# A hybrid block's first feed-forward: other load order, bank sharing, copy places and block sums at its head

## The chip, the cores and the metric

The kernel runs on one core of one Trainium2 chip. The metric is the device time of one execution in microseconds (us). Before the change it was 1982.98 us, the median of three runs (1982.03 to 1984.27). All details below come from one further, profiled execution.

## The reference

One layer works on 1040 tokens of 1024 values: 16 meta tokens and 1024 frames. Everything is float32.

```python
h = concat([meta, x])
h = h + 0.5 * swiglu(rmsnorm(h, ffn1_norm), ffn1_w_gate, ffn1_w_up, ffn1_w_down)
u = rmsnorm(h, mix_norm); P = u @ w_in
ya = window_sink_attention(...)         # from parts of P
yb = gated_linear_attention(...)        # from other parts of P
h = h + (sigmoid(gate_a) * (ya @ w_branch_att) + sigmoid(gate_b) * (yb @ w_branch_gla)) @ w_out
h = h + 0.5 * swiglu(rmsnorm(h, ffn2_norm), ffn2_w_gate, ffn2_w_up, ffn2_w_down)
return rmsnorm(h, final_norm)[16:]

def swiglu(x, w_gate, w_up, w_down):
    return (silu(x @ w_gate) * (x @ w_up)) @ w_down
```

The change touches only the beginning of the first feed-forward: its norm and its products with `w_gate` and `w_up` (1024 x 2816 each, so 22 column blocks of 128, numbered 0 to 21).

## The kernel before

**Arithmetic.** Each float32 operand is split into a high half (rounded to the matmul's format, by ScalarE) and a low half (what is left, by VectorE), and each product is three matmuls: high by high, high by low, low by high. A feature dimension of 1024 is eight parts of 128, numbered m or k. Weights are cut the same way: `plain_cut` writes `whi` on ScalarE (L220) and `wlo` on VectorE or, where it is told so, on GpSimd (L221).

**Column blocks 1 to 19** are made by `gate_up` with seven products for eight (a scheme like Strassen's): 24 matmuls per product, each product on sums of blocks of weights (`s` L455, `wop` L233 and L234) and of tokens. The token side has four blocks, B11 to B22, and four sums of them, T1 to T4, which `token_sums` makes once: subtractions in place in `ub` (L251 to L253, L257) and then their halves `tt` (L233, L234). After each product `pump` takes one piece of work out of the list `pending`, and lets `spare` do a turn of work for later phases: `w_out` and the first weight sums of the second feed-forward. The product results lie in tiles `pa`, `pb`, `pd` of two PSUM banks each.

**Column blocks 20 and 21** (the head) and block 0 are made plainly. The tokens form four chunks q = 0 to 3 of 256, 264, 256 and 264. Chunk 0 needs the token tiles x0 and x1, chunk 1 needs x2, x3 and the meta tokens (x8). The head is written out in a fixed order for SyncE's queue (SP), ScalarE (ACT), VectorE (DVE) and TensorE (PE):
- SP issues the loads: token tiles, block 20's weights in four pieces (`raw`, L532), block 21's weights in two (`rawx`, L212).
- `turn_x(q, m)` turns the chunk's tiles for one feature part with TensorE into a PSUM bank (`xps`, L573 and L575). For chunk 0 the parts m and m+1 share a bank; for other chunks each part has its own.
- `first_put` (chunks 0 and 1) reads that bank three times: ACT writes the high half `tb` (L585), DVE the low half (L588), and a raw copy goes to `ub`, by ACT for odd m (L587) and by DVE for even m (L590). Behind chunk 1's part the raw copy of both chunks is written to memory.
- `head_products(q, ...)` runs 16 steps for one column block and chunk, eight parts for the gate and eight for the up weights, three matmuls each (L650 to L652), into banks `pg` and `pu`. For block 20 gate and up steps alternate, for block 21 all gate steps come first. Ahead of a step, hooks from a table run other pieces: `put` (turn and halve one part of a later chunk), `square_x` (sum of squares of one token tile), `root` (their reciprocal roots, spread by a GpSimd copy, L621 to L623), `spread` (these turned into rows by TensorE, L631), `emptied` (results out of the banks, L660), `cut` (block 21's weights).

Behind the head a scheduler orders the work by itself. `more(0, ...)` makes block 0 for the chunks 2, 3, 0, 1; its results leave the banks in four `finish` steps (`m` on DVE, L760), which `token_sums` calls at four places through `between`. Then the pool of single banks is closed and two pools of two-bank tiles are opened over the same memory; the first product of `gate_up(1)` (`pb`, L472) is the first to write there.

Of the kernel before, what the change touches and what calls it, by code (L numbers as in the profile page):

```python
# [15 lines left out]
PSUM = bass.MemoryType.PSUM  # L16

P = 128
# [17 lines left out]
def hybrid_kernel(  # L36
# [136 lines left out]
    class Seven:  # L173
# [72 lines left out]

        def token_sums(self, ub, between=None):

            b11, b21, b12, b22 = ub[0][0:4], ub[0][4:8], ub[1][0:4], ub[1][4:8]
            for k in range(4):  # L250
                nc.vector.tensor_sub(b11[k], b12[k], b11[k])  # L251
                nc.vector.tensor_sub(b12[k], b22[k], b12[k])
                nc.vector.tensor_sub(b22[k], b22[k], b11[k])  # L253
            for n, bs in (("T2", b22), ("T1", b11), ("T3", b12), ("T4", b21)):
                for k in range(4):
                    if n == "T4":
                        nc.vector.tensor_sub(b21[k], b21[k], b22[k])  # L257
                    self.tops[n][k] = self.halves(self.operand(False, "tt"), bs[k])
                    if between is not None:
                        between(n, k)  # L260

# [32 lines left out]
        def pump(self):  # L294
            free = not self.pending
            if self.pending:
                self.pending.pop(0)()
            if self.spare:
                self.spare.turn(free and self.at > 1)
            self.at = (self.at + 1) % 7  # L300
# [233 lines left out]

    head_raw(0, 0)
    load_x(1, nc.sync)
    for i, k in ((1, 0), (0, 4), (1, 4)):
        head_raw(i, k)
    load_x(2, nc.sync)
    load_x(3, nc.sync)  # L540
    nc.sync.dma_start(out=xt[8][0:NM, :], in_=meta_tokens)
    head_raws += [ffn1.plain_raw(cols_view(w, HEADS[1] * P), r) for w, r in zip((ffn1_w_gate, ffn1_w_up), extra)]
    for t in range(4, 8):
# [17 lines left out]
    def turn_x(q, m):  # L561

        c, c0, n = CH[q]
        sl = slice(m * P, (m + 1) * P)
        if q == 0:
            if m % 2 == 0:
                pairs[m // 2] = bank("xps")
            ps = pairs[m // 2][:, (m % 2) * 256:(m % 2) * 256 + 256]
        else:
            ps = bank("xps")  # L570
        if n > 256:
            at = 256 - 8 * c
            nc.tensor.transpose(ps[:, at:at + NM], xt[8][0:NM, sl], ident[0:NM, 0:NM])  # L573
        for i in range(2):
            nc.tensor.transpose(ps[:, i * P:(i + 1) * P], xt[4 * c + c0 // P + i][:, sl], ident)  # L575
        return ps[:, 0:n]

    def first_put(q, m, ps):

        c, c0, n = CH[q]  # L580
        if c0 == 0:
            ub[0][m], B[0][m] = ffn1.block("ub"), ffn1.operand(True, "tb")
        g, cols = vec[:, G1 + m:G1 + m + 1], slice(c0, c0 + n)
        hi, lo = B[0][m][:, cols], B[0][m][:, N1 + c0:N1 + c0 + n]
        nc.scalar.activation(hi, ps, AF.Copy, scale=g)  # L585
        if m % 2:
            nc.scalar.copy(ub[0][m][:, cols], ps)  # L587
        nc.vector.scalar_tensor_tensor(lo, ps, g, hi.bitcast(F32), op0=ALU.mult, op1=ALU.subtract)  # L588
        if m % 2 == 0:
            nc.vector.tensor_copy(ub[0][m][:, cols], ps)  # L590
        if c0:
            nc.sync.dma_start(out=x_dram[0, m], in_=ub[0][m])

# [102 lines left out]
    def put(q, m):  # L696
        def go():
            ps = turn_x(q, m)
            if q < 2:
                first_put(q, m, ps)  # L700
            else:
# [17 lines left out]

    turned = [turn_x(0, m) for m in range(KT)]  # L720
    for m in range(KT):
        first_put(0, m, turned[m])
        if m in (0, 3):
            cuts[0][m // 3]()
            cuts[1][m // 3]()
    hooks = {
        (0, 0): {6: [cut(1, 0, nc.gpsimd)], 8: [do(square_x, 1, eng=v)], 10: [cut(1, 1)], 12: [put(1, 0)], 14: [put(1, 1)]},
        (0, 1): {0: [do(root, 0), put(1, 2)], 2: [put(1, 3)], 4: [put(1, 4)], 6: [put(1, 5)], 8: [put(1, 6)], 10: [put(1, 7)],
                 12: [do(spread, 0)], 13: [do(square_x, 8, NM), do(square_x, 2, eng=v)]},
        (1, 0): {0: [emptied(0, 0)], 1: [do(square_x, 6)], 2: [do(square_x, 3, eng=v)], 4: [emptied(1, 0)],  # L730
                 5: [do(square_x, 7)], 6: [do(square_x, 4, eng=v)], 9: [do(root, 1)], 10: [do(square_x, 5, eng=v)],
                 13: [do(root, 2), do(root, 3)]},
        (1, 1): {0: [do(spread, 1)], 1: [emptied(0, 1)], 7: [do(spread, 2), do(spread, 3)],
                 **{8 + m: [put(2, m)] for m in range(KT)}},
# [28 lines left out]
    def between(n, k):  # L763
        if (n, k) in (("T2", 1), ("T2", 3), ("T1", 3), ("T3", 3)):
            ends.pop(0)()
# [6 lines left out]
    dbl.update(down=False, a=ExitStack(), b=ExitStack())  # L772
    dbl["pools"] = [dbl[x].enter_context(tc.tile_pool(name=f"psd{x}", bufs=1, space=PSUM, side=side))
                    for x, side in (("a", "right"), ("b", "left"))]
# [1285 lines left out]
```

## Time and profile before

| | |
|---|---|
| median of the runs | 1982.98 us |
| lowest, highest | 1982.03, 1984.27 us |
| the profiled execution, its own time | 1982.2 us |
| its span, first to last instruction | 1980.4 us |
| mean granted TensorE clock | 0.998 |
| TensorE idle in all | 18.7 us |
| TensorE's first matmul of chunk 1 | at 31.13 us |
| its first seven-product matmul | at 97.09 us |

The span is what the rows of the profile cover; 1.8 us of the execution lie around it. The lists of waits read "engine, tile and line waited, for what: us in total, times, longest". A row of the timeline gives the start in the span, the time until its end, the engine, the line, the operation, result and operands with their shape, the count of neighbours taken together, and in brackets how long the engine stood idle before and for whom. The rows of a query by tile give minimum, median and maximum duration in ns, the first and last start, and for DMAs the us from issue to landing. A row by stretches gives for one stretch of time its length, then the busy time and instruction count of TensorE, of its weight loads (PEld), DVE, ACT and POOL (GpSimd), the granted clock, the DMA share and GB/s.

### The profile page before, as it was taken

The page shows a single profiled execution, that of the slowest core. Times are in us where ns is not written, and L with a number is a line of the kernel's source. Part 1 is how long each engine was busy: PE and PEld are TensorE (multiplying, and loading weights), DVE is VectorE, ACT ScalarE, POOL GpSimd, SP SyncE. Part 2 cuts the span into 40 slices and gives each one's busy share as a digit, 9 for nine tenths or more (in the row PEclk, how much of TensorE's full clock was granted, in tenths as well). Part 3 has the DMA queues.
Part 4 walks back from the last instruction along what each step waited for, and adds up shares of the span by engine and source line. Part 5 has one row for each costly group of instructions (what it writes and reads, how often), then busy time and mean ns, then how long its engine had stood idle before and what let it go on. Part 6 is the DMA issues. An engine that isn't in the chain of part 4 may idle for free. (4 is left out here: it accounts for less than half of the span.)

```text
span 1980.4 us, 32143 instructions
## 1 busy us (share of the span) xinstructions
PE 1961.7 (99%) x11892; PEld 1741.4 (88%) x11892; DVE 1452.7 (73%) x2563; ACT 910.4 (46%) x1794; POOL 151.7 (8%) x185
## 2 busy tenths in 40 slices
PE   8999999999999999999999999999999999999998
PEld 8999999999999988888889878888888888888887
DVE  6988887777678776566566657869767767767886
ACT  5555454554322255465456535425444444442225
POOL 1000000001323100003300000000000000022220
PEclk9999999999999999999999999999999999999999
DMA  6377776779776233356621546985534534588732
GB/s 215 107 239 239 251 259 224 262 264 347 266 271 224 86 130 109 112 159 212 194 62 52 168 164 215 299 304 173 178 128 149 190 129 132 200 302 324 280 102 86
DMA packets 299613, 386.47 MB, mean 195 GB/s; under 512 B 28854, under 2 KB 187312, under 8 KB 299456
## 3 DMA queue, kind: packets, MB, share of 16 engines
q1 hardware_dynamic: 283824, 330.41, 50.4%
q10 hardware_dynamic: 15280, 53.89, 7.5%
q8 instruction: 94, 1.54, 0.3%
q0 software_dynamic: 352, 0.11, 0.1%
q14 instruction: 63, 0.52, 0.1%
HBM read 245.77 MB, written 138.57 MB: 194 GB/s over the span
## 5 line engine op out<-in xcount | busy, mean ns | idle before, releaser
L472 PE MATMUL pb<-tt,wop 128*128 128x260 f32 (+1 forms) x2244 | 384.7, 325 | 0.0
L472 PEld LDWEIGHTS pb<-tt,wop 128*128 128x128 f32 x2244 | 333.0, 188 | 34.7 <-DVE u L332 0.4
L233 ACT CAST wop<-s 128x512 fp32r<-128x512 f32 x264 | 163.5, 621 | 239.8 <-PE pb L472 92.0
L234 DVE TENSOR_TENSOR wop<-s,wop 128x512 fp32r<-128x512 f32 x264 | 185.4, 703 | 75.1 <-ACT wop L233 74.7
L472 PE MATMUL pb<-tm,wop 128*128 128x260 f32 (+1 forms) x1440 | 233.7, 318 | 0.0
L472 PEld LDWEIGHTS pb<-tm,wop 128*128 128x128 f32 x1440 | 207.1, 188 | 18.7
L233 ACT CAST wop<-raw 128x512 fp32r<-128x512 f32 x198 | 122.7, 621 | 191.6 <-PE pb L472 95.6
L472 PE MATMUL pd<-tt,wop 128*128 128x512 f32 (+1 forms) x1008 | 190.0, 341 | 0.0
L472 PEld LDWEIGHTS pd<-tt,wop 128*128 128x128 f32 x1008 | 159.4, 188 | 21.5
L234 DVE TENSOR_TENSOR wop<-raw,wop 128x512 fp32r<-128x512 f32 x198 | 137.4, 696 | 32.2 <-ACT wop L233 32.0
L352 DVE SCALAR_TENSOR_TENSOR h<-pb,h 128x520 f32<-128x520 f32 (+1 forms) x136 | 94.1, 693 | 37.7 <-PE pb L472 35.8
L472 PE MATMUL pd<-tm,wop 128*128 128x260 f32 (+1 forms) x720 | 118.8, 319 | 0.0
L455 POOL TENSOR_TENSOR s<-raw 128x512 f32<-128x512 f32 x28 | 37.5, 1339 | 1019.0 <-DVE wop L234 542.9
L472 PE MATMUL pb<-tb,wop 128*128 128x260 f32 (+1 forms) x684 | 112.4, 318 | 0.8 <-DVE m L760 0.8
L472 PEld LDWEIGHTS pd<-tm,wop 128*128 128x128 f32 x720 | 104.3, 188 | 9.3
L472 PE MATMUL pa<-tb,wop 128*128 128x260 f32 (+1 forms) x684 | 112.1, 317 | 0.0
L455 DVE TENSOR_TENSOR s<-raw 128x512 f32<-128x512 f32 x90 | 62.0, 688 | 61.7 <-DMA raw<-in_ffn_w_up 57.8
L472 PEld LDWEIGHTS pb<-tb,wop 128*128 128x128 f32 x684 | 98.6, 188 | 9.8 <-ACT vec L87 0.9
L472 PEld LDWEIGHTS pa<-tb,wop 128*128 128x128 f32 x684 | 98.5, 188 | 8.9
L96 PE MATMUL pj<-uh,whi 128*128 128x512 f32 (+2 forms) x256 | 91.5, 357 | 0.0
L98 PE MATMUL pj<-uh,wlo 128*128 128x512 f32 (+2 forms) x256 | 90.0, 352 | 0.4 <-DVE wlo L126 0.4
L97 PE MATMUL pj<-ul,whi 128*128 128x512 f32 (+2 forms) x256 | 89.8, 351 | 0.0
(439 smaller groups left out, 3795.0 us busy)
## 6 DMA issues: line engine op xcount, KB each, us to landing
tm<-f1mid ACTq DMA_DIRECT2D x49, 520.0 KB, 5.5
tm<-f2mid ACTq DMA_DIRECT2D x49, 512.0 KB, 4.7
raw<-in_ffn_w_down SPq DMA_DIRECT2D x80, 256.0 KB, 4.8
raw<-in_ffn_w_gate SPq DMA_DIRECT2D x39, 512.0 KB, 4.0
raw<-in_ffn_w_up SPq DMA_DIRECT2D x39, 512.0 KB, 4.2
f1mid<-kh SPq DMA_DIRECT2D x63, 260.0 KB, 4.3
f1mid<-kl SPq DMA_DIRECT2D x63, 260.0 KB, 4.1
f2mid<-kh SPq DMA_DIRECT2D x63, 256.0 KB, 2.8
```

Of the source, the lines that this page charges most:

```text
L96: nc.tensor.matmul(ps, wh[k], xh[k], start=(k == 0), stop=False)
L97: nc.tensor.matmul(ps, wh[k], xl[k], start=False, stop=False)
L98: nc.tensor.matmul(ps, wl[k], xh[k], start=False, stop=(k == n - 1))
L233: nc.scalar.copy(x[:, 0:n], src)
L234: nc.vector.tensor_sub(x[:, n:2 * n], src, x[:, 0:n].bitcast(F32))
L352: nc.vector.scalar_tensor_tensor(hm, ps, 0.5, hm, op0=ALU.mult, op1=ALU.add)
L455: (eng.tensor_add if add else eng.tensor_sub)(a[s], a[x], a[y])
L472: nc.tensor.matmul(ps, y, z[:, s0:s0 + sn], start=(first and k == 0 and at == 0), stop=(at == 2 and k == len(cols) - 1), skip_group_check= ...
```

## The change

1. SP's loads come in another order: both token tiles of chunk 0 first, then block 20's weights, then block 21's gate weights, x2, block 21's up weights, x3 and the meta tokens.
2. In chunk 0 the parts m and m+4 share a bank.
3. `first_put` returns its raw copy as a function. For chunk 0 all eight are done at one later place; for chunk 1 at once as before.
4. Block 21's gate weights are cut on DVE, not on GpSimd. The hooks move: cuts, raw copies, chunk 1's eight puts, `root`, `spread`, `emptied`.
5. `token_sums` cuts only T2 and T1 at once. T3 and T4 go into `pending`, in six pieces that run between the products of `gate_up(1)`. The `finish` steps stand at other places.
6. `pump` lets `spare` turn one product earlier in a block in which nothing is pending.
7. The pools of two-bank tiles get `reuse_waits="tile"`: a tile waits for those earlier tiles that it overlaps, not for the whole closed pool.

The instructions are the same but for one cut's engine; 3 and the table of hooks move most of them.

```diff
-        def token_sums(self, ub, between=None):
+        def token_sums(self, ub, between):
...
-            for n, bs in (("T2", b22), ("T1", b11), ("T3", b12), ("T4", b21)):
+            def cut(n, k, src):
+                self.tops[n][k] = self.halves(self.operand(False, "tt"), src[k])
+
+            for n, bs in (("T2", b22), ("T1", b11)):
                 for k in range(4):
-                    if n == "T4":
-                        nc.vector.tensor_sub(b21[k], b21[k], b22[k])
-                    self.tops[n][k] = self.halves(self.operand(False, "tt"), bs[k])
-                    if between is not None:
-                        between(n, k)
+                    cut(n, k, bs)
+                    between(n, k)
+
+            def fourth(ks):
+                for k in ks:
+                    nc.vector.tensor_sub(b21[k], b21[k], b22[k])
+                    cut("T4", k, b21)
+
+            self.pending += [lambda k=k: cut("T3", k, b12) for k in range(4)] + [lambda k=k: fourth((k, k + 1)) for k in (0, 2)]
...
-                self.spare.turn(free and self.at > 1)
+                self.spare.turn(free and self.at > 0)
...
-            if m % 2 == 0:
-                pairs[m // 2] = bank("xps")
-            ps = pairs[m // 2][:, (m % 2) * 256:(m % 2) * 256 + 256]
+            if m < 4:
+                pairs[m] = bank("xps")
+            ps = pairs[m % 4][:, (m // 4) * 256:(m // 4) * 256 + 256]
...
-        if m % 2:
-            nc.scalar.copy(ub[0][m][:, cols], ps)
         nc.vector.scalar_tensor_tensor(lo, ps, g, hi.bitcast(F32), op0=ALU.mult, op1=ALU.subtract)
-        if m % 2 == 0:
-            nc.vector.tensor_copy(ub[0][m][:, cols], ps)
-        if c0:
-            nc.sync.dma_start(out=x_dram[0, m], in_=ub[0][m])
+
+        def keep():
+            if m % 2:
+                nc.scalar.copy(ub[0][m][:, cols], ps)
+            else:
+                nc.vector.tensor_copy(ub[0][m][:, cols], ps)
+            if c0:
+                nc.sync.dma_start(out=x_dram[0, m], in_=ub[0][m])
+        return keep
...
-        (0, 0): {6: [cut(1, 0, nc.gpsimd)], 8: [do(square_x, 1, eng=v)], 10: [cut(1, 1)], 12: [put(1, 0)], 14: [put(1, 1)]},
-        (0, 1): {0: [do(root, 0), put(1, 2)], 2: [put(1, 3)], 4: [put(1, 4)], 6: [put(1, 5)], 8: [put(1, 6)], 10: [put(1, 7)],
-                 12: [do(spread, 0)], 13: [do(square_x, 8, NM), do(square_x, 2, eng=v)]},
-        (1, 0): {0: [emptied(0, 0)], 1: [do(square_x, 6)], 2: [do(square_x, 3, eng=v)], 4: [emptied(1, 0)],
+        (0, 0): {6: [cut(1, 0)], 9: keeps, 12: [do(square_x, 1, eng=v), cut(1, 1)]},
+        (0, 1): {2: [put(1, 0)], 3: [do(root, 0)], 4: [put(1, 1)], 6: [put(1, 2)], 7: [put(1, 3)], 8: [put(1, 4)],
+                 9: [put(1, 5)], 10: [put(1, 6)], 12: [put(1, 7)], 14: [do(square_x, 8, NM), do(square_x, 2, eng=v)]},
+        (1, 0): {0: [do(spread, 0), do(square_x, 6)], 2: [emptied(0, 0), do(square_x, 3, eng=v)], 4: [emptied(1, 0)],
...
-        (1, 1): {0: [do(spread, 1)], 1: [emptied(0, 1)], 7: [do(spread, 2), do(spread, 3)],
+        (1, 1): {4: [do(spread, 1)], 5: [emptied(0, 1)], 7: [do(spread, 2), do(spread, 3)],
...
-        if (n, k) in (("T2", 1), ("T2", 3), ("T1", 3), ("T3", 3)):
+        if (n, k) in (("T2", 1), ("T2", 3), ("T1", 2), ("T1", 3)):
...
-    dbl["pools"] = [dbl[x].enter_context(tc.tile_pool(name=f"psd{x}", bufs=1, space=PSUM, side=side))
+    dbl["pools"] = [dbl[x].enter_context(tc.tile_pool(name=f"psd{x}", bufs=1, space=PSUM, side=side, reuse_waits="tile"))
```

The first loads on SP's queue, before the change:

```order
L507 DMA x0_106<-in_x 128x1024
L532 DMA raw_141<-in_ffn1_w_gate 128x4x128
L507 DMA x1_107<-in_x 128x1024
L532 DMA raw_142<-in_ffn1_w_up 128x4x128
L532 DMA raw_141<-in_ffn1_w_gate 128x4x128
L532 DMA raw_142<-in_ffn1_w_up 128x4x128
L507 DMA x2_108<-in_x 128x1024
L507 DMA x3_109<-in_x 128x1024
L541 DMA x8_114<-in_meta_tokens 16x1024
L212 DMA rawx_120<-in_ffn1_w_gate 128x8x128
L212 DMA rawx_121<-in_ffn1_w_up 128x8x128
```

The same place on SP's queue after the change (lines stand seven or more lower):

```order
L514 DMA x0_106<-in_x 128x1024
L514 DMA x1_107<-in_x 128x1024
L539 DMA raw_141<-in_ffn1_w_gate 128x4x128
L539 DMA raw_142<-in_ffn1_w_up 128x4x128
L539 DMA raw_141<-in_ffn1_w_gate 128x4x128
L539 DMA raw_142<-in_ffn1_w_up 128x4x128
L212 DMA rawx_120<-in_ffn1_w_gate 128x8x128
L514 DMA x2_108<-in_x 128x1024
L212 DMA rawx_121<-in_ffn1_w_up 128x8x128
L514 DMA x3_109<-in_x 128x1024
L549 DMA x8_114<-in_meta_tokens 16x1024
```

x1 moved ahead of the first weights; x3 and the meta tokens moved behind all of block 21's weights; the eleven loads are the same.

On DVE, the second half of chunk 0 before the change: low halves (`tb`) and raw copies (`ub`) of the parts 4 to 7, the squares of x1, and the low half of block 21's up weights:

```order
L588 SCALAR_TENSOR_TENSOR tb_221<-xps_182,vec_84,tb_221 128x256
L590 COPY ub_220<-xps_182 128x256
L588 SCALAR_TENSOR_TENSOR tb_226<-xps_182,vec_84,tb_226 128x256
L588 SCALAR_TENSOR_TENSOR tb_231<-xps_187,vec_84,tb_231 128x256
L590 COPY ub_230<-xps_187 128x256
L588 SCALAR_TENSOR_TENSOR tb_236<-xps_187,vec_84,tb_236 128x256
L557 ISA sqx_270,xs_122<-x1_107 128x1024
L557 ISA xs_122 128x1
L221 TENSOR_TENSOR wlo_279<-rawx_121,whi_278 128x1024
```

The same stretch of DVE after the change:

```order
L593 SCALAR_TENSOR_TENSOR tb_217<-xps_172,vec_84,tb_217 128x256
L593 SCALAR_TENSOR_TENSOR tb_221<-xps_175,vec_84,tb_221 128x256
L593 SCALAR_TENSOR_TENSOR tb_225<-xps_178,vec_84,tb_225 128x256
L593 SCALAR_TENSOR_TENSOR tb_229<-xps_181,vec_84,tb_229 128x256
L221 TENSOR_TENSOR wlo_253<-rawx_120,whi_252 128x1024
L599 COPY ub_192<-xps_172 128x256
L599 COPY ub_204<-xps_178 128x256
L599 COPY ub_216<-xps_172 128x256
L599 COPY ub_224<-xps_178 128x256
L564 ISA sqx_282,xs_122<-x1_107 128x1024
L564 ISA xs_122 128x1
L221 TENSOR_TENSOR wlo_285<-rawx_121,whi_284 128x1024
```

The low halves stand in a row, each from another bank than its neighbour; the cut of block 21's gate weights (`wlo_253`) is new on this engine; the raw copies stand behind both.

On DVE at the hand-over from block 0 to block 1 before the change: halves `tt` of the token sums, the last two results `m` of block 0, the sums `ub` for T4, block 1's weights `wop` and `s`:

```order
L234 TENSOR_TENSOR tt<-ub,tt 128x520 x8
L760 TENSOR_TENSOR m_1267<-pu,a 128x256
L257 TENSOR_TENSOR ub<-ub 128x520 x3
L234 TENSOR_TENSOR tt<-ub,tt 128x520 x3
L257 TENSOR_TENSOR ub<-ub 128x520
L234 TENSOR_TENSOR wop<-raw,wop 128x512 x2
L760 TENSOR_TENSOR m_1267<-pu,a 128x264
L234 TENSOR_TENSOR tt<-ub,tt 128x520
L455 TENSOR_TENSOR s<-raw 128x512
```

And after the change:

```order
L462 TENSOR_TENSOR s<-raw 128x512
L771 TENSOR_TENSOR m_1264<-pu,a 128x256
L462 TENSOR_TENSOR s<-s,raw 128x512
L462 TENSOR_TENSOR s<-raw 128x512
L462 TENSOR_TENSOR s<-raw,s 128x512
L234 TENSOR_TENSOR tt<-ub,tt 128x520
L234 TENSOR_TENSOR wop<-s,wop 128x512
L234 TENSOR_TENSOR tt<-ub,tt 128x520
L234 TENSOR_TENSOR wop<-s,wop 128x512
L234 TENSOR_TENSOR tt<-ub,tt 128x520
L234 TENSOR_TENSOR wop<-s,wop 128x512
L771 TENSOR_TENSOR m_1264<-pu,a 128x264
```

Block 1's weight sums moved ahead of the last `m`, and most halves of T3 and T4 with their sums behind it.

More of the change, by code (lines that the diff above doesn't have):

```diff
@@ L533, in head_raw @@
                           in_=w[k * P:(k + 4) * P, HEADS[0] * P:(HEADS[0] + 1) * P].rearrange("(k p) m -> p k m", p=P))
-    head_raw(0, 0)
     load_x(1, nc.sync)
-    for i, k in ((1, 0), (0, 4), (1, 4)):
+    for i, k in ((0, 0), (1, 0), (0, 4), (1, 4)):
         head_raw(i, k)
+    head_raws += [ffn1.plain_raw(cols_view(ffn1_w_gate, HEADS[1] * P), extra[0])]
     load_x(2, nc.sync)
+    head_raws += [ffn1.plain_raw(cols_view(ffn1_w_up, HEADS[1] * P), extra[1])]
     load_x(3, nc.sync)
     nc.sync.dma_start(out=xt[8][0:NM, :], in_=meta_tokens)
-    head_raws += [ffn1.plain_raw(cols_view(w, HEADS[1] * P), r) for w, r in zip((ffn1_w_gate, ffn1_w_up), extra)]
     for t in range(4, 8):
@@ L699, in go @@
             if q < 2:
-                first_put(q, m, ps)
+                first_put(q, m, ps)()
             else:
@@ L720, in hybrid_kernel @@
     turned = [turn_x(0, m) for m in range(KT)]
+    keeps = []
     for m in range(KT):
-        first_put(0, m, turned[m])
+        keeps.append(first_put(0, m, turned[m]))
         if m in (0, 3):
```

## The prediction

> **What bounds the kernel now.** First the busy times of part 1 of the page, then the list of TensorE's waits, then TensorE's timeline around them.
>
> ```profile
> PE 1961.7 (99%) x11892; PEld 1741.4 (88%) x11892; DVE 1452.7 (73%) x2563; ACT 910.4 (46%) x1794; POOL 151.7 (8%) x185
> ...
> PE xps L575 <- DMA x<-in_x: 2.8, 1, 2.8
> PE pg L652 <- POOL wlo L221: 1.3, 1, 1.3
> ...
> PE pg L651 <- DVE tb L588: 0.8, 2, 0.4
> ...
> PE pb L472 <- DVE m L760: 0.8, 1, 0.8
> ```
>
> The span is 1980.4 us and the profiled execution took 1982.2 us. TensorE (PE) is busy for all but 18.7 us of it, so only what shortens its idle time, or the time in which its matmuls stand further apart than they need, moves the end. The first three waits lie in the first 31 us, the last at 97 us; all four are at places that the change edits. The change removes no matmul, so it can win only there.
>
> ```profile
> 8.37 2.88 PE L575 MATMUL xps<-ident,x 128*128 128x128 f32 x15 [2.80 <-DMA x<-in_x]
> ...
> 17.93 0.28 PE L652 MATMUL pu<-tb,wlo 128*128 128x256 f32 x1
> 18.14 0.24 PE L573 MATMUL xps<-ident,x 16*128 16x16 f32 x1
> ...
> 21.18 0.28 PE L651 MATMUL pg<-tb,whi 128*128 128x256 f32 x1
> 22.71 0.38 PE L652 MATMUL pg<-tb,wlo 128*128 128x256 f32 x1 [1.25 <-POOL wlo L221]
> ...
> 23.73 0.36 PE L650 MATMUL pg<-tb,whi 128*128 128x256 f32 x1
> ...
> 24.97 0.36 PE L650 MATMUL pg<-tb,whi 128*128 128x256 f32 x1
> ...
> 30.06 0.28 PE L650 MATMUL pu<-tb,whi 128*128 128x256 f32 x1
> ...
> 31.13 0.28 PE L650 MATMUL pg<-tb,whi 128*128 128x264 f32 x1
> ```
>
> The first token chunk has 32 steps of three matmuls, 16 for column block 20 and 16 for block 21. By 17.93 twelve are done; at 18.14 the first put of the second chunk is turned; at 31.13 the second chunk's products begin. Three steps without anything between take from 30.06 to 31.13, **0.357 us a step**. From 23.73 to 24.97 are two steps and one put, so **0.526 a put**.
>
> **The head, part by part.** Where do the twelve steps lose time? In the hand-over between ScalarE (ACT) and VectorE (DVE):
>
> ```profile
> 12.70 0.47 ACT L585 ACTIVATE tb<-xps,vec 128x256 fp32r<-128x256 f32 x1 [1.16 <-DVE ub L590]
> ...
> 18.05 0.47 ACT L585 ACTIVATE tb<-xps,vec 128x256 fp32r<-128x256 f32 x1 [0.90 <-DVE ub L590]
> ```
>
> ```profile
> 10.26 1.28 DVE L221 TENSOR_TENSOR wlo<-raw,whi 128x512 fp32r<-128x512 f32 x2
> 11.46 0.87 DVE L588 SCALAR_TENSOR_TENSOR tb<-xps,vec,tb 128x256 fp32r<-128x256 f32 x2
> 13.47 0.48 DVE L588 SCALAR_TENSOR_TENSOR tb<-xps,vec,tb 128x256 fp32r<-128x256 f32 x1 [0.81 <-ACT ub L587]
> ...
> 18.82 0.48 DVE L588 SCALAR_TENSOR_TENSOR tb<-xps,vec,tb 128x256 fp32r<-128x256 f32 x1 [0.81 <-ACT ub L587]
> ```
>
> ACT waits for DVE's raw copy out of the same bank, then DVE for ACT's, to and fro; the last low half starts at 18.82. With parts m and m+4 in one bank and the raw copies behind all halves, neighbours stand in different banks and these waits go. What is late next? The eight low halves on DVE, some 0.41 each, and four weight cuts of 0.62 each: 5.8 us. They begin later than now: a bank's first reader waits for ten transposes, not four, but x1 is asked for earlier.
>
> ```profile
> L507 SPq DMA_DIRECT2D x<-in_x x1: 497/497/497, 1.7 to 1.7; - x1
> ...
> DMA to landing us min/median/max: 6.6/6.6/6.6
> ```
>
> ```profile
> L212 SPq DMA_DIRECT2D rawx<-in_ffn_w_gate x1: 973/973/973, 7.0 to 7.0; - x1
> ...
> DMA to landing us min/median/max: 9.4/9.4/9.4
> ...
> L212 SPq DMA_DIRECT2D rawx<-in_ffn_w_up x1: 2457/2457/2457, 8.3 to 8.3; - x1
> ...
> DMA to landing us min/median/max: 9.8/9.8/9.8
> ```
>
> Token tile x1 lands at 1.7 + 6.6 = 8.3 and the last of the eleven first loads, the second block's up weights, at 8.3 + 9.8 = 18.1, 1.7 behind the gate weights at 7.0 + 9.4 = 16.4. Those are 512 KB; the load of 256 KB that no longer stands ahead of x1 is half of that, 0.9: an estimate of 7.4 for x1 (bounds 6.6 and 8.3, a whole such load and none). Now ACT starts at 9.0, 0.7 behind x1's landing; six transposes more, 15 of which take 2.88 us, are 1.1, so it starts at some 9.2 and DVE at 9.7, and the last low half is out at 15.5. The products of block 20 end at some 17.0 (two more steps and the hand-over between the engines), the low half of block 21's gate weights (1.2) is ready at 16.8, and after two steps of block 21 TensorE would turn the second chunk's first part at 17.7.
>
> That put needs x2, x3 and the meta tokens. The first eleven loads are the same set as before, and the meta tokens are now their last: they land where the up weights did, 18.1. So **TensorE waits some 0.4 us for meta** and then stands at 18.15 with 18 steps done, against twelve now. Left are 14 steps of 0.357 (5.0), eight puts of 0.526 (4.2) and 0.25 for the transposes of `spread`, which stood inside this stretch and now stand right behind it: 27.6 against 31.13, **a gain of 3.5 us**. Two parts of it: six steps more by 18.14 (2.1), and the wait for POOL at 22.71 (1.4 from step to step).
>
> Is that wait replaced by one for DVE, which now does both cuts?
>
> ```profile
> 19.83 2.83 POOL L221 TENSOR_TENSOR wlo<-rawx,whi 128x1024 fp32r<-128x1024 f32 x1 [15.18 <-ACT whi L220]
> ...
> 20.71 3.02 DVE L221 TENSOR_TENSOR wlo<-rawx,whi 128x1024 fp32r<-128x1024 f32 x1 [0.26 <-ACT whi L220]
> ...
> 67.88 1.22 DVE L221 TENSOR_TENSOR wlo<-raw,whi 128x1024 fp32r<-128x1024 f32 x1 [1.98 <-ACT whi L220]
> ```
>
> The same DVE cut takes 1.22 alone and 3.02 beside POOL, which ends at 22.66: 1.8 us longer. Two cuts alone are 2.44, so DVE gets 0.6 us lighter by taking POOL's share. By the two durations added up (1.22 more for DVE) the cut would cost instead: DVE's queue ahead of the puts would be 1.8 longer than I take it, of which the 0.4 of waiting for meta hides a part; the gain would fall to some 2.1. I take the row, since the 3.02 is measured beside POOL alone. The Trainium skill, "SBUF — State Buffer", section "Who interferes with whom", says that a VectorE operation with two SBUF inputs and a GpSimd instruction that reads SBUF hold the shared port by turns, the later one blocked for the whole instruction. By that rule POOL's going takes the whole 1.8 with it, which gives the sum that I make by the row; the trace agrees, as the second cut began 0.88 after the first and ended 1.07 after it.
>
> Behind 27.6 everything up to 96 us is set by TensorE and moves with it. `spread` of the second chunk stands four steps later and has room; a wait there would be 0 to 0.5 us, and I take 0.
>
> **The hand-over at 97 us.**
>
> ```profile
> 90.71 0.42 DVE L760 TENSOR_TENSOR m<-pu,a 128x256 f32<-128x256 f32 x1
> ...
> 95.31 1.28 DVE L234 TENSOR_TENSOR wop<-raw,wop 128x512 fp32r<-128x512 f32 x2
> 96.52 0.43 DVE L760 TENSOR_TENSOR m<-pu,a 128x264 f32<-128x264 f32 x1
> ```
>
> ```profile
> 97.09 3.11 PE L472 MATMUL pb<-tb,wop 128*128 128x260 f32 x24 [0.81 <-DVE m L760]
> ```
>
> The first product of column block 1 waits until all single banks are closed, that is for the fourth `m` at 96.52. With waits by tile it waits only for the one it lies over, the third (90.71, and earlier after the change); the fourth is needed by the fourth product. **Gain 0.8**; if DVE still came late, 0. The queue on DVE is shorter too, since 8 halves and 4 sums of T3 and T4 (some 0.62 each, like the two cuts at 95.31: 7.4 us) move behind it.
>
> ```profile
> 76.00:97.00 21.00, 20.28 (x169) 20.04 (x167) 21.00 (x38) 10.62 (x21) 0.00 (x0) 1.00 0.24 86
> 97.00:137.00 40.00, 39.91 (x333) 39.94 (x334) 33.39 (x54) 20.68 (x37) 0.00 (x0) 1.00 0.80 259
> 137.41:157.88 20.47, 20.45 (x171) 20.23 (x170) 18.06 (x30) 9.43 (x18) 0.00 (x0) 1.00 0.54 175
> 157.88:178.90 21.02, 20.90 (x171) 20.31 (x170) 19.35 (x33) 10.73 (x20) 0.00 (x0) 1.00 0.93 309
> ```
>
> In these rows of stretches (length, busy time of PE, weight loads, DVE, ACT, POOL, clock, DMA) DVE is full until 97 and has 6.6 us free in the two column blocks behind. T3 is wanted by the fourth product and T4 by the fifth of block 1, at some 101 and 104 (92.8 and three or four products of 2.9); DVE, which stood full before, is done with them by 99.5, since it comes to block 1 some 3.5 earlier and 7.4 us are only moved. No wait. But block 3 took 20.47 and block 4 took 21.02, where two blocks in 97 to 137 took 20.1 each: **DVE is nearly full there, and matmuls stand 1.25 us further apart in all**. The spare work now starts one product earlier in each block that has nothing pending (`at > 0`) and lies otherwise; this loss may go or double, 0 to -1.3 or +1.3. I take -0.5, since the work before is spread more evenly.
>
> **Sum:** -3.5 - 0.8 - 0.5 = -4.8, from 1982.2 to 1977.4. The median of the runs shown, 1982.98, lies 0.8 above the profiled execution, so the time is **1978.2**, its own range 1976.8 to 1979.4.
>
> **The rivals.**
>
> Tokens later than 18.1. x3 and meta now follow 1 MB of weights; if they land at 19 to 20, TensorE waits for them and every us is lost in full: gain 2.6 to 1.6 in the head, 1979.1 to 1980.1. For it: SP's issue of the last weights alone takes 2.457 us. Against: before, loads landed in order of issue.
>
> Tokens at 17.0, and the stretched matmuls of blocks 3 and 4 gone: TensorE then sets the put's time itself, 17.7, and the gain is 3.5 + 0.4 + 0.8 + 1.25, so 1977.0.
>
> The clock.
>
> ```profile
> 5.00:10.00 5.00, 2.20 (x13) 1.89 (x14) 0.47 (x2) 2.20 (x6) 0.00 (x0) 0.90 0.99 256
> 10.00:15.00 5.00, 4.94 (x31) 4.64 (x29) 4.16 (x10) 3.69 (x10) 0.00 (x0) 0.76 1.07 330
> ```
>
> The granted clock is 0.90 in 5 to 10 us and 0.76 in 10 to 15: at half clock that is 1.0 us before 10 and 2.4 behind it, so from 9.0 to 12.4, behind the wait for x1. A second such window would cost up to 1.7 us of the steps in it; since the 0.4 of waiting for meta cover a part, some 1.3: 1979.5. The Trainium skill, "TensorE: Matmul & The Clock Gate", section "What's actually happening", has a free-running window of about 3.4 us that decides the rate. The 9 to 12.4 agree with it; where the window lies in another run, no row shows.
>
> The other side: DVE starves the products. In block 4 it is busy 19.35 of 21.02 and the block takes 0.9 longer than 20.1. If one spare turn more per block brings each of the nine odd blocks from 3 on to that state, 8.1 us are added to -4.3: 1982.98 + 3.8, **1986.8**. It decides as soon as DVE has under 1.7 us free in such a block. Against: the spare work is the same in amount, so what is done earlier is missing later.
>
> The change not doing what it says: the wait by tile might not be shortened at 97 (the 0.8 stays, 1979.0).
>
> **How the numbers follow.** Under 0.2% (4.0 us, about what a measurement of this kernel can tell from no change) means above 1979.0. Chances: forecast 0.48 (0.42 below 1979.0), early tokens 0.14, late tokens 0.18 (0.03 below), clock or wait at 97 left 0.12 (0.03 below), starved products 0.08. So faster 0.62, same 0.31, slower 0.07. The range from 1975.5 to 1982.0 leaves out the starved products and a little at the lower end, and holds spread of some 1 us between executions.
>
> **What would show it.** Right: no wait of `tb` L585 on the raw copy and none on POOL in the first 20 us; the first 128x264 product near 27.6; the first `pb` product right behind the turned vectors, at some 92.8; blocks 3 and 4 at 20.1 to 21.0. Wrong: meta as TensorE's longest wait in the head, of over 1.5 us; a wait for `racc`'s operands; blocks of over 21 us in a row.

## The result, and the profile after

The changed kernel takes 1979.06 us, the median of 11 runs (1976.50 to 1982.32); the kernel before took 1982.98 in 11 runs beside it. The ratio is 0.9979, 95% interval 0.9969 to 0.9988: 3.9 us or 0.2% faster, and the interval leaves out 1. The forecast was 1978.2, range 1975.5 to 1982.0. The profiled execution took 1978.71 us with a span of 1976.9, 3.5 less than before.

TensorE's waits up to 31 us, in the same list as before:

```profile
PE xps L580 <- DMA x<-in_meta_tokens: 1.4, 1, 1.4
...
PE xps L582 <- DMA x<-in_x: 0.6, 1, 0.6
PE pg L660 <- ACT whi L220: 0.5, 1, 0.5
PE pg L662 <- DVE wlo L221: 0.2, 1, 0.2
PE pg L661 <- DVE tb L593: 0.2, 1, 0.2
```

The wait for x1 fell from 2.8 to 0.6, the one for POOL is gone, and the wait for the meta tokens is the new longest one. The timeline of TensorE at the same places:

```profile
5.94 1.86 PE L582 MATMUL xps<-ident,x 128*128 128x128 f32 x15 [0.65 <-DMA x<-in_x]
...
15.97 0.28 PE L662 MATMUL pg<-tb,wlo 128*128 128x256 f32 x1
17.63 0.23 PE L580 MATMUL xps<-ident,x 16*128 16x16 f32 x1 [1.39 <-DMA x<-in_meta_tokens]
...
26.87 0.37 PE L660 MATMUL pg<-tb,whi 128*128 128x264 f32 x1
...
92.10 3.13 PE L479 MATMUL pb<-tb,wop 128*128 128x260 f32 x24
...
478.58 3.05 PE L479 MATMUL pb<-tm,wop 128*128 128x260 f32 x24
```

Chunk 1's products (the marker of the tests below) begin at 26.87 instead of 31.13, **4.26 earlier**. The first seven-product matmul begins at 92.10 instead of 97.09, **4.99 earlier**: 4.26 from the head and 0.87 from the hand-over (from the last product of block 0 to it are 0.38 instead of 1.25), less 0.14 lost between the two. The last row is the first product of the down projection, behind column block 19; before the change its row reads

```profile
480.70 3.02 PE L472 MATMUL pb<-tm,wop 128*128 128x260 f32 x24
```

so only **2.12** of the 4.99 are left there: the 19 blocks took 386.48 us (478.58 - 92.10) instead of 383.61. The starts of the blocks' first matmuls, read from the same timelines, show where:

| blocks, us from one block's first matmul to the next's | before | after |
|---|---|---|
| 1 and 2 | 20.20, 20.12 | 20.21, 20.10 |
| 3 and 4 | 20.47, 21.02 | 20.10, 20.10 |
| 5 to 9 | 20.12 each | 20.10, 20.81, 20.51, 21.56, 20.10 |
| 10 to 17 | 20.12 each | 20.34, then 20.10 to 20.12 |
| 18 and 19 | 20.12, 20.12 | 20.52, 21.32 |

The stretched blocks 3 and 4 became good and gave 1.3; blocks 6, 7, 8, 10, 18 and 19 went bad and took 4.3. Of the last 1.4 us of the span's gain, 0.9 lie between 1150 and 1160 us, in a phase that the change doesn't touch. In the profile of another kernel with that phase unchanged (the one below with only the spare turn edited) it is also 0.9 shorter than in the profile before, so this is no gain of the change.

What stretched block 8? DVE's row in its timeline, and how its weights were loaded:

```profile
243.85 0.69 DVE L462 TENSOR_TENSOR s<-raw 128x512 f32<-128x512 f32 x1 [3.09 <-DMA raw<-in_ffn_w_up]
```

```profile
225.10 1.35 SPq L817 DMA_DIRECT2D woS<-pr  x3
226.79 0.76 SPq L817 DMA_DIRECT2D woS<-ph  x1
227.61 3.93 SPq L817 DMA_DIRECT2D woS<-pr  x3
231.59 1.42 SPq L808 DMA_DIRECT2D pr<-in_w_out  x3
233.06 0.99 SPq L808 DMA_DIRECT2D pr<-in_ffn_w_up  x2
234.15 1.20 SPq L808 DMA_DIRECT2D pr<-in_ffn_w_gate  x2
235.39 2.66 SPq L313 DMA_DIRECT2D raw<-in_ffn_w_up  x1
```

DVE was not full there: it stood idle for 3.09 us for block 8's up weights. SP's queue had put 14 transfers of spare work (`woS`, `pr`) ahead of them in ten microseconds; the weights' own issue took 2.66 us and they were used at 243.85, 8.5 after it began. `s` came late, and with it the high half of `wop` on ACT; behind that in ACT's queue stood the copy of a result out of its bank (L333), for which TensorE waited:

```profile
246.52 3.14 PE L479 MATMUL pb<-tt,wop 128*128 128x260 f32 x24 [0.85 <-ACT g L333]
```

Blocks 7 and 19 show a late load as well (ACT waited 4.20 us for block 7's gate weights, DVE 6.75 for a load in block 19, and TensorE 0.94 for the same copy there); what made these late was not followed. In block 6 DVE ran without a pause from 197.65 to the end, with pieces of spare work (`pr`) between its own. Over the blocks 6, 7 and 8 the rows of stretches (length, PE, weight loads, DVE, ACT, POOL, clock) are

```profile
192.70:213.51 20.81, 20.64 (x170) 20.23 (x169) 18.71 (x32) 10.96 (x20) 0.00 (x0) 1.00 0.84 293
213.51:234.02 20.51, 20.37 (x171) 20.16 (x169) 15.85 (x25) 9.65 (x17) 0.00 (x0) 1.00 0.70 228
234.02:255.58 21.56, 20.64 (x171) 20.23 (x169) 16.88 (x28) 9.95 (x18) 0.00 (x0) 1.00 0.90 279
```

So DVE had 2.1 us free in block 6, 4.7 in the blocks 7 and 8, and 3.4 to 10.2 in the blocks 10, 18 and 19.

### The profile page after: what moved, and what is told of

It is laid out like the page before. It is cut to its first block, busy times and chain, and to the rows that moved or that the text cites. A ratio compares the mean times of both kernels' runs of the same rounds, so it can differ in the third digit from the quotient of the medians.

```text
span 1976.9 us, 32153 instructions
## 1 busy us (share of the span) xinstructions
PE 1959.5 (99%) x11892; PEld 1739.9 (88%) x11892; DVE 1451.5 (73%) x2564; ACT 909.0 (46%) x1794; POOL 148.7 (8%) x184
## 5 line engine op out<-in xcount | busy, mean ns | idle before, releaser
L479 PE MATMUL pb<-tt,wop 128*128 128x260 f32 (+1 forms) x2244 | 384.5, 325 | 2.2 <-ACT g L333 1.8
```

The costliest lines, as they stand in the source:

```text
L479: nc.tensor.matmul(ps, y, z[:, s0:s0 + sn], start=(first and k == 0 and at == 0), stop=(at == 2 and k == len(cols) - 1), skip_group_check= ...
```

## The experiments

The times are medians, and each ratio is to runs of the kernel before that were made beside them; the last three columns are from the profiles (blocks 1 to 19 as above). For e10 there is one execution and no ratio.

| run | median us (runs) | ratio, 95% interval | marker | first seven-product | blocks 1 to 19 |
|---|---|---|---|---|---|
| before | 1982.98 (11) | | 31.13 | 97.09 | 383.61 |
| changed | 1979.06 (11) | 0.9979, 0.9969 to 0.9988 | 26.87 | 92.10 | 386.48 |
| e1, old loads | 1982.13 (10) | 0.9997, 0.9988 to 1.0007 | 28.64 | 94.44 | 385.23 |
| e2, neighbours share banks | 1981.98 (10) | 0.9994, 0.9984 to 1.0003 | 27.08 | 93.80 | 388.28 |
| e3, copies at once | 1984.28 (10) | 1.0004, 0.9995 to 1.0013 | 31.53 | 97.39 | 387.14 |
| e4, cut on GpSimd | 1979.37 (10) | 0.9982, 0.9973 to 0.9992 | 26.83 | 92.05 | 388.59 |
| e5, changed with at > 1 | 1981.40 (11) | 0.9984, 0.9975 to 0.9993 | 26.17 | 91.40 | 382.63 |
| e8, before with at > 0 | 1986.69 (11) | 1.0012, 1.0003 to 1.0021 | 31.29 | 97.16 | 387.51 |
| e6, tokens first | 1980.60 (10) | 0.9982, 0.9973 to 0.9991 | 27.27 | 92.95 | 384.34 |
| e7, no waits by tile | 1979.62 (10) | 0.9982, 0.9973 to 0.9991 | 26.94 | 92.86 | 386.54 |
| e9, two pieces | 1976.26 (6) | 0.9968, 0.9956 to 0.9979 | 26.21 | 91.44 | 384.53 |
| e11, changed again | 1978.97 (11) | 0.9976, 0.9967 to 0.9985 | 26.45 | 91.67 | 387.22 |
| e12, two pieces again | 1978.06 (8) | 0.9972, 0.9961 to 0.9982 | 26.70 | 91.92 | 384.47 |
| e10, no spare turns | 2088.71 (1) | | 26.82 | 92.05 | 382.01 |

The marker of the changed kernel moves by 0.4 between its own two profiles (26.87 and 26.45), so smaller differences of it say nothing.

**Undoing parts of the head.** The first run took back the order of loads:

```diff
-    load_x(1, nc.sync)
-    for i, k in ((0, 0), (1, 0), (0, 4), (1, 4)):
+    head_raw(0, 0)
+    load_x(1, nc.sync)
+    for i, k in ((1, 0), (0, 4), (1, 4)):
...
```

> The changed kernel with the old order of loads. Marker: the first 128x264 product, 26.87 us in the changed kernel's profile, 31.13 before. Theory A (banks, late copies and hooks carry most of the head's gain, the load order some): x1 lands at about 8.3 instead of 5.9, so block 20's products start 2.4 later; the meta tokens are early, so the wait of 1.4 for them goes: marker at 27.9. Theory B (the load order is the gain): marker near 30. The rest of the span alike: total 1 us (A) or 3 us (B) above the changed kernel.

The marker is 28.64: 1.8 lost, between the two but nearer to A. TensorE's turns of chunk 0, in its timeline:

```profile
8.12 3.46 PE L582 MATMUL xps<-ident,x 128*128 128x128 f32 x15 [2.55 <-DMA x<-in_x]
```

The 15 transposes take 3.46 us here and 1.86 in the changed kernel, and the matmuls behind them start 0.21 apart until 14.0, then 0.12. With x1 late TensorE stands idle for 2.55 us and then runs at half speed, though this profile's row of the granted clock says 1.00 there; the spacing decides. So it is in all three profiles with the old order of loads (2.88 us for the 15 transposes in the kernel before, 3.46 in e1 and e8). With x1 early it is so in three of eleven (e6, e10 and e12 below, 3.46 each, behind only 0.4 to 0.7 us of idle time), and the other eight have 1.86. The order of loads may thus bring more than the earlier landing, as half speed seems rarer with it, but it does not rule half speed out. Against that the wait for meta, which would have hidden part of the loss, is gone with the old order.

The whole time is 3.1 us above the changed kernel's, which is what theory B had said. In the profiles e1 is only 1.1 behind at the end of block 19 (479.67 and 478.58) and 3.1 at the end of the span; the rest lies in phases that the edit does not touch and stays unexplained.

The second run let neighbours share a bank again:

```diff
-            if m < 4:
-                pairs[m] = bank("xps")
-            ps = pairs[m % 4][:, (m // 4) * 256:(m // 4) * 256 + 256]
+            if m % 2 == 0:
+                pairs[m // 2] = bank("xps")
+            ps = pairs[m // 2][:, (m % 2) * 256:(m % 2) * 256 + 256]
```

> The changed kernel with parts m and m+1 sharing a bank again, raw copies still late. Theory A (the shared bank makes ACT and DVE wait for each other): ACT's high half of an odd part waits for DVE's low half of the even one, some 0.8 to 1.2 us in each of four pairs; block 20's products end 2 to 3 us later, of which the wait for meta (1.4) hides a part: marker 27.9 to 28.5. Rival (only the raw copies made them wait): marker 26.9, no such waits.

The waits came back (A), three of four and of 0.58 to 0.86, and the marker moved by only 0.21, as the rival had it. ACT's rows:

```profile
10.09 0.47 ACT L592 ACTIVATE tb<-xps,vec 128x256 fp32r<-128x256 f32 x1 [0.81 <-DVE tb L593]
...
12.83 0.84 ACT L592 ACTIVATE tb<-xps,vec 128x256 fp32r<-128x256 f32 x2 [0.86 <-DVE tb L593]
14.25 0.47 ACT L592 ACTIVATE tb<-xps,vec 128x256 fp32r<-128x256 f32 x1 [0.58 <-DVE tb L593]
```

All of the delay fitted under the wait for the meta tokens: the put of chunk 1's first part starts at 17.64 here and at 17.63 in the changed kernel. DVE stays 2.0 us behind, though (its first low half of chunk 1 at 20.78 instead of 18.78), and TensorE pays later: by the first seven-product matmul 1.7 us are lost. Two waits of TensorE behind the marker, 0.3 for a raw copy on DVE and 0.5 at the hand-over, are half of that; the rest was not followed. A marker that lies right behind a wait hides what the wait covers.

The third run made the raw copies at once:

```diff
-        keeps.append(first_put(0, m, turned[m]))
+        first_put(0, m, turned[m])()
...
-        (0, 0): {6: [cut(1, 0)], 9: keeps, 12: [do(square_x, 1, eng=v), cut(1, 1)]},
+        (0, 0): {6: [cut(1, 0)], 12: [do(square_x, 1, eng=v), cut(1, 1)]},
```

> The changed kernel with chunk 0's raw copies made at once, banks still shared by m and m+4. Theory A (the copies cost only their own durations once neighbours stand in different banks): DVE and ACT get 4 x 0.41 and 4 x 0.36 us in front of the halves, 1.4 to 1.6, and the wait for meta hides nearly all of it: marker 26.9 to 27.3. Rival (the copies are what made the engines wait): marker 28.5 to 29, with waits of 0.8 to 1.2 on the copies.

The rival was right, and more: 31.53, all of the head's gain lost and the kernel as slow as before. ACT's rows:

```profile
10.16 0.37 ACT L597 COPY ub<-xps 128x256 f32<-128x256 f32 x1 [1.08 <-DVE tb L593]
10.43 0.84 ACT L592 ACTIVATE tb<-xps,vec 128x256 fp32r<-128x256 f32 x2
12.18 0.37 ACT L597 COPY ub<-xps 128x256 f32<-128x256 f32 x1 [0.91 <-DVE tb L593]
```

A raw copy waits for DVE's low half of its own part. Other neighbours do not help there; only the place of the copy does. Each of ACT's four copies stood 0.9 to 1.2 us and the next high halves behind it. By the time chunk 1 was turned (20.88 instead of 17.63) the wait for meta was used up. Then the clock fell; the rows of stretches (length, PE, weight loads, DVE, ACT, POOL, clock) are

```profile
15.00:20.00 5.00, 3.81 (x25) 3.07 (x25) 2.80 (x6) 3.38 (x6) 0.00 (x0) 1.00 1.04 375
20.00:25.00 5.00, 4.80 (x24) 4.13 (x25) 3.73 (x8) 1.51 (x4) 0.39 (x1) 0.66 1.14 325
```

A clock of 0.66 in 5 us is 3.4 us at half speed, up to 1.7 us lost.

The fourth run gave block 21's gate cut back to GpSimd:

```diff
-        (0, 0): {6: [cut(1, 0)], 9: keeps, 12: [do(square_x, 1, eng=v), cut(1, 1)]},
+        (0, 0): {6: [cut(1, 0, nc.gpsimd)], 9: keeps, 12: [do(square_x, 1, eng=v), cut(1, 1)]},
```

> The changed kernel with block 21's gate weights cut on GpSimd again. Theory A (the split cost by holding up DVE's own cut; now that cut runs 3 us later, and the loads set the pace): POOL's cut takes 2.8 from about 13.8 to 16.6, TensorE wants it at 15.6, the wait for meta stands until 17.6 anyway: marker 26.9 to 27.2. Rival (the split is bad by itself): marker 28 or later, DVE operations beside it lengthened to 2 us or more.

Theory A: marker 26.83. TensorE waited 0.23 for POOL at 15.85 and 0.4 less for meta behind it. The rival's other sign came too, one DVE operation of 2.11 us beside POOL (the last section has it), but it cost the marker nothing. Taking the split away costs or brings nothing in the new arrangement: before, the two cuts lay side by side (19.83 to 22.66 and 20.71 to 23.73), here they don't.

**The wait for meta.** One kernel loads x3 and the meta tokens ahead of block 21's up weights, and cuts those behind the second put:

```diff
     load_x(2, nc.sync)
-    head_raws += [ffn1.plain_raw(cols_view(ffn1_w_up, HEADS[1] * P), extra[1])]
     load_x(3, nc.sync)
     nc.sync.dma_start(out=xt[8][0:NM, :], in_=meta_tokens)
+    head_raws += [ffn1.plain_raw(cols_view(ffn1_w_up, HEADS[1] * P), extra[1])]
...
-        (0, 0): {6: [cut(1, 0)], 9: keeps, 12: [do(square_x, 1, eng=v), cut(1, 1)]},
-        (0, 1): {2: [put(1, 0)], 3: [do(root, 0)], 4: [put(1, 1)], 6: [put(1, 2)], 7: [put(1, 3)], 8: [put(1, 4)],
+        (0, 0): {6: [cut(1, 0)], 9: keeps, 12: [do(square_x, 1, eng=v)]},
+        (0, 1): {2: [put(1, 0)], 3: [do(root, 0)], 4: [put(1, 1), cut(1, 1)], 6: [put(1, 2)], 7: [put(1, 3)], 8: [put(1, 4)],
```

> The changed kernel with x3 and the meta tokens loaded ahead of block 21's up weights, and these weights cut behind the second put. Theory A (the wait of 1.4 us for the meta tokens is all that holds TensorE there): that wait goes, marker (first 128x264 product) at 25.4 to 25.8 instead of 26.87, total 1.0 to 1.4 lower up to 97 us. Rival (the up weights, then last to land at 17.6, or ACT and DVE behind them, hold it instead): a wait for wlo or whi of over 0.7 appears, marker 26.5 or later.

The wait for meta went and the marker did not move forward: 27.27. But this execution ran at half speed at its start, with x1 in time:

```profile
6.25 3.46 PE L582 MATMUL xps<-ident,x 128*128 128x128 f32 x15 [0.67 <-DMA x<-in_x]
```

Its last product of block 20 started 1.1 later than in the changed kernel (16.37 and 15.26). In e10 and e12, whose head is the changed kernel's, half speed delayed it by 1.0 and 0.8, and a wait for meta of 0.3 and 0.4 was left behind it; here nothing stood behind to hide the delay. A wait of 0.5 for the low half of the up weights stood among the later puts, less than the rival's 0.7. So the test does not decide between the two: how much of the 1.4 us this order of loads would bring at full speed is open.

**The hand-over at 92 us.** The seventh kernel is without the waits by tile:

```diff
-... name=f"psd{x}", bufs=1, space=PSUM, side=side, reuse_waits="tile"))
+... name=f"psd{x}", bufs=1, space=PSUM, side=side))
```

> The changed kernel with the two-bank pools waiting for the whole closed pool again. Theory A (the wait for the last m is then back): the first seven-product matmul waits for the m at 92.23 and starts at 92.7 to 92.9 instead of 92.10, a loss of 0.6 to 0.8. Rival (the reordered DVE queue alone had removed that wait): it starts at 92.1 to 92.2.

Theory A, in the row

```profile
92.86 3.11 PE L479 MATMUL pb<-tb,wop 128*128 128x260 f32 x24 [0.63 <-DVE m L771]
```

The wait for the last `m` is back with 0.63, so the waits by tile bring that much of the 0.87 gained at the hand-over (from the last product of block 0 to this one are 1.08, against 0.38 with them). In the whole time, 1979.62 against 1979.06, it can't be told apart.

**The spare work.** One edit, in the changed kernel (back to the old value) and in the kernel before (to the new one):

```diff
-                self.spare.turn(free and self.at > 0)
+                self.spare.turn(free and self.at > 1)
```

> The changed kernel with the spare work's turn one product later again (at > 1), the rest of the change kept. In the changed kernel the column blocks 6 to 9 take 83.0 us together instead of 80.5 before, and blocks 3 and 4 40.2 instead of 41.5. Theory S (the earlier turn puts bursts of spare transfers ahead of a block's weights, which then land late): blocks 6 to 9 take 80.5 again, the stall of 0.85 us in block 8 goes, blocks 3 and 4 may lose up to 1.3; total 1 to 2.5 us below the changed kernel's 1979. Rival (that blocks 3 to 9 lie 5 us earlier against the transfers, whatever the turn): blocks 6 to 9 still at 82.5 to 85.

> The kernel before with one edit: the spare work's turn one product earlier (at > 0). Theory S: blocks 6 to 9 take 82.5 to 85 us instead of 80.5, blocks 3 and 4 40.2 to 40.5 instead of 41.5; total 1 to 3 us above the kernel before. Rival: all blocks as before, total the same.

For the blocks taken together theory S holds in both directions. With at > 1 blocks 3 to 9 take 20.10 each; with at > 0 in the kernel before, all 19 blocks take 3.9 us more (387.51) and the ratio is 1.0012, with 1 outside its interval. It missed the place: there blocks 3 and 4 went bad (22.69 and 21.70), not 6 to 9. It missed e5's total as well: the gain in the blocks did not reach the end, and the ratio of 0.9984 is no better than the changed kernel's 0.9979 and 0.9976. In the profile e5 is 4.5 us ahead of the changed kernel at the first product of the down projection (474.03) and 4.0 behind at the end. TensorE behind block 19 and SP's queue there:

```profile
476.89 3.03 PE L479 MATMUL pa<-tm,wop 128*128 128x260 f32 x24
479.76 0.88 PE L479 MATMUL pb<-tm,wop 128*128 128x260 f32 x6
485.95 4.27 PE L479 MATMUL pb<-tm,wop 128*128 128x260 f32 x18 [5.31 <-DMA tm<-f1mid]
```

```profile
471.55 0.61 SPq L369 DMA_DIRECT2D tm<-f1mid  x1
475.70 0.34 SPq L817 DMA_DIRECT2D gu20A<-ph  x1
...
477.34 0.39 SPq L817 DMA_DIRECT2D gu21A<-pr  x1
477.79 10.81 SPq L369 DMA_DIRECT2D tm<-f1mid  x9
```

The last spare jobs (`gu20A`, `gu21A`) were not done when the blocks ended. They stand in SP's queue ahead of the loads of the down projection's operands, wait there for their own data until 475.7, and nine loads wait behind them: 5.31 us of TensorE, and half speed behind it (18 matmuls in 4.27). So the earlier turn (at > 0) is no separate tuning. T3 and T4, in six pieces of `pending`, take six of block 1's seven turns, and five of the seven were the spare work's before; the earlier turn gives it one more in each odd block from 3 on.

Three more runs follow from this. The first leaves block 1 its turns: T3 and T4 in two pieces, and at > 1.

```diff
-            self.pending += [lambda k=k: cut("T3", k, b12) for k in range(4)] + [lambda k=k: fourth((k, k + 1)) for k in (0, 2)]
+            self.pending += [lambda: [cut("T3", k, b12) for k in range(4)], lambda: fourth(range(4))]
...
-                self.spare.turn(free and self.at > 0)
+                self.spare.turn(free and self.at > 1)
```

> The changed kernel with T3 and T4 put off in two pieces instead of six and the spare turn at at > 1 as before: block 1 then has five free turns again, as many as before the change, and all spare work stands ahead of the down products' loads. Theory (six pieces take block 1's free turns; at > 0 makes up for them at the price of 3 us of stretched products in blocks 6 to 9, and at > 1 alone leaves two spare jobs that hold up the loads at 476 us): no wait of over 2 us at 470 to 490; blocks 3 to 9 take 140.7 to 142 us together (seven of 20.1; before 142.1, changed kernel 143.3, with at > 1 alone 140.7); total 1976 to 1978.5, 1 to 3 us below the changed kernel in the same call. Rival (any arrangement of the spare work costs the same somewhere): blocks 3 to 9 at 143 or more, or a new wait before 490, total as the changed kernel.

> The kernel with T3 and T4 in two pieces and the spare turn at at > 1, again, since its first times were only six. If its gain of some 2.7 us over the changed kernel (1976.26 against 1978.97 in one call) is real, the median is 1975.5 to 1977.5 and the ratio to the kernel before 0.9960 to 0.9975; blocks 3 to 9 take 142 to 142.5 us together, block 19 20.1 instead of the changed kernel's 21.3, and no wait stands between 470 and 490 us. If it was chance, the median is at 1978.5 or above and block 19 at 21 or more.

The wait at 480 is gone, and blocks 5 to 19 take 20.10 to 20.14 each. Blocks 2 to 4 are stretched now (21.10, 20.50, 21.20 in the first profile), so blocks 3 to 9 took 142.22 there, 0.2 above what the theory gave at most, and 141.83 in the second, 0.2 below what was expected of it; over all 19 blocks it is 384.5 in both profiles, 2 us less than in the changed kernel. The times are 1976.26 and 1978.06. The second lies between the two medians that were expected of it; its ratio (0.9972) and block 19 (20.10) are as expected if the gain is real. Its profile lay 0.4 us behind the first's at the end of block 19 and 5.5 at the end of the span; 3.9 of these came around 1285 us, with the row

```profile
1280.00:1290.00 10.00, 8.03 (x29) 6.16 (x28) 9.32 (x15) 4.23 (x8) 0.00 (x0) 0.83 0.99 346
```

a half-speed window behind an idle stretch, in a phase that none of these kernels changes. All 14 runs of the two have a median of 1977.6, the 22 of the changed kernel 1979.0. The ratios' intervals overlap: the medians differ by 1.4 us, 0.4 to 2.8 in 95% of cases when the runs are drawn again at random. So this version is likely a little better than the changed kernel, and clearly faster than the one before.

> The changed kernel again, for a second profile and for times beside those of the kernels of this call. If the stretched products of blocks 6 to 9 come from the order of the spare work, they take 82 to 85 us together again (83.0 in the first profile); if they were chance, 80.5 to 81. The head's marker at 26.2 to 27.0, the first seven-product matmul at 91.4 to 92.2.

Blocks 6 to 9 took 83.47 again (20.91, 21.36, 21.08, 20.12), so the stretch belongs to the order of the work and is not chance. Some of it is: block 14 took 20.92 here and 20.10 in the first profile.

The last run takes the two lines with `spare.turn` out of `pump`.

> The changed kernel without any spare turn between products; all spare work runs in one piece between block 19 and the down products (the output is the same). Theory S (spare work, its DVE time and its transfers, is what stretches blocks 3 to 9): blocks 2 to 19 take 20.10 each, with no wait; a wait of some 30 us or more follows behind block 19. Rival (the blocks' own weights and results are enough to stretch them): blocks 6 to 9 still over 81 together. The total says nothing, it is far above.

Theory S: every block from 2 on takes 20.10, and 109.4 us of waiting follow. The blocks' own weights and results stretch nothing. Since this takes away the spare work's DVE operations together with its transfers, no run here parts the two.

## Why the prediction held, point by point

**The head, -3.5 forecast, -4.26 measured.** The steps held: chunk 1's first put with 18 steps done, no waits of the halves on raw copies, none on POOL, meta as what TensorE waits for. Both of block 21's cuts on DVE take 1.22 to 1.23 us, so the 3.02 of before went with POOL, as the forecast took it. Two terms were mis-sized. Token tile x1 was estimated at 7.4 (bounds 6.6 to 8.3) and landed at 5.9:

```profile
L514 SPq DMA_DIRECT2D x<-in_x x1: 420/420/420, 1.2 to 1.2; - x1
...
DMA to landing us min/median/max: 4.7/4.7/4.7
```

The estimate took the distance between two loads at the end of the queue for that at its start, and even its bound was too late. And meta landed at 11.0 + 6.6 = 17.6, not 18.1. With 17.63 in place of 18.15 the sum gives 27.1; measured 26.87. The wait for meta became 1.4 instead of 0.4, because everything ahead of it came earlier. The forecast gave over 1.5 as a sign of being wrong, so this was close to it.

**Which part carried it.** The forecast gave 2.1 to the steps and 1.4 to the wait for POOL, and spoke of banks and copies together. The runs part them: copies at once cost 4.7 of the marker (up to 1.7 of it by half speed), the order of loads 1.8 (half speed in it too), neighbours in one bank 0.2 there and 1.7 by 92 us, POOL's split nothing. They don't add up, since each loss first fills the wait for meta.

**The clock rival** forecast a second half-speed window from the wait for meta. None came in the changed kernel's two profiles, and the window of before was gone from them as well. That this was the change's doing is not shown: e10 and e12 have the changed kernel's head and ran its start at half speed. Each stretch at half speed named here (before, e1, e3, e5 at 480, e6, e8, e10, e12 at its start and at 1285) stands behind or in a stretch with idle time, but idle time alone does not decide: 0.4 to 0.9 us ahead of the 15 transposes brought half speed in three profiles and none in eight. The Trainium skill, "TensorE: Matmul & The Clock Gate", section "What's actually happening", has a window of 3413 ns whose activity decides the rate; the 3.4 us of e3 agree with it. The 1.39 us of idle time at 16 us, in a stretch with TensorE busy for 3.6 of 5 us, brought no such window, while 3.5 and 3.8 of 5 us in e3 did. What decides between these is open.

**The hand-over, -0.8 forecast, -0.87 measured,** by the mechanism given: e7 shows 0.63 of it to be the waits by tile.

**The column blocks, -0.5 forecast (0 to -1.3 or +1.3), +2.87 measured.** This step failed, in size and in reason. The forecast looked at DVE's load and at blocks 3 and 4, which did come right (-1.3). It held that spare work done earlier is missing later, so that the blocks lose nothing. What it did not see is that T3 and T4 take the turns in block 1 that the spare work had, and that the spare work with its turns moved stretches six later blocks by 4.3 us; e5, e8 and e10 show that it is the spare work. In block 8 it acts through SP's queue, where a burst of its transfers delays the block's weights. Whether the other five go by the queue or by DVE's order of work is open. The rival of starved products had the sign, but it had nine blocks and 8.1 us, and it needed DVE with under 1.7 us free in a block; DVE had at least 2.1 in each of the six. "Blocks of over 21 us in a row" was a sign of being wrong; blocks 8 and 19 are over 21, but not in a row.

**The sum** came out right within 0.9 us by luck, because errors of opposite sign met: -0.8 in the head, +3.4 in the blocks, and in the profiles another -1.4 behind block 19, of which 0.9 are chance. Profile against profile (1978.71 against the 1977.4 that the sum gave) it is 1.3 too low; the median of the changed kernel lies 0.4 above its profile, not 0.8.

## What to carry to other kernels

Work that is moved into free slots takes them from the work that ran there; ask who used the slots, and what waits at the end if that isn't done in time. In a queue that issues in order, a burst of uncritical transfers can make a critical one late, with engines idle beside it (DVE for 3.09 us in block 8, TensorE for 5.31 us in e5). Behind a wait that covers everything, undoing a part looks free at the next marker; measure it at a later one too.

## What the runs showed of the hardware

Half speed of TensorE came and went with one and the same head: with that of the changed kernel the 15 transposes took 1.86 us in five profiles (changed, e5, e7, e9, e11) and 3.46 in two (e10, e12). In e1, e6, e8, e10 and e12 the row of the granted clock said 1.00 there, and only the spacing of the matmuls (0.21 instead of 0.12 us) showed it. Half speed came behind idle stretches also far from the start (e12 lost 3.9 us around 1285 us, idle time and half speed together), and may so explain a part of the 3 to 7 us by which runs of one kernel differ; only single executions were profiled.

With GpSimd's cut (13.40 to 15.80) in e4, DVE's sum of squares beside it took longer, and DVE's copies out of the banks did not:

```profile
13.40 2.40 POOL L221 TENSOR_TENSOR wlo<-rawx,whi 128x1024 fp32r<-128x1024 f32 x1 [8.74 <-ACT whi L220]
```

```profile
13.45 1.41 DVE L599 COPY ub<-xps 128x256 f32<-128x256 f32 x4
14.78 2.11 DVE L564 CUSTOM_DVE_ANT_0 sqx<-x 128x1024 bf16<-128x1024 f32 x1
```

The four copies take 1.41 with and without POOL beside them; the squares take 2.11 instead of 1.22 and end 1.1 behind POOL. The Trainium skill, "SBUF — State Buffer", section "Who interferes with whom", has this contention for VectorE operations with two SBUF inputs. The squares read one tile twice, and they fit; the copies read PSUM alone.
